# Two transposes two steps later, start-up tables in the mixing's memory, and a split last scatter in a two-layer encoder

## The chip, the cores and the metric

The kernel runs on one core of one Trainium2 chip. A core has TensorE (PE in the profile; PEld is its weight load), VectorE (DVE), ScalarE (ACT), GpSimd (POOL), SyncE (SP, which here only issues transfers) and 16 DMA engines. The metric is the device time of one execution in microseconds (us), from its start to its end, taken as the median of several runs.

## The reference

The reference is a streaming encoder of two layers (`DEPTH = 2`) over 256 tokens of width 1024, one sequence, all in float32. Each layer does this, cut to what matters:

```
mod = silu(c) @ w_ada[i] + b_ada[i]                 # 6 x 1024: sh1, sc1, g1, sh2, sc2, g2
h   = rmsnorm(x, norm1_g) * (1 + sc1) + sh1
q_a,k_a,v_a,u_s,q_r,k_r,v_r,g_r = split(h @ w_in)    # 1024 -> 2816 columns
y_a = chunk-banded attention, 8 heads, clipped relative bias
y_s = S5: complex diagonal recurrence over the tokens, discretised from
      a_re, a_im, exp(log_dt), then gelu and a GLU
y_r = 4-head retention with rotary angles, group norm, silu gate
x   = x + g1 * (concat(y_a, y_s, y_r) @ w_out)
h   = rmsnorm(x, norm2_g) * (1 + sc2) + sh2
x   = x + g2 * moe(h)      # 32 experts in 4 groups; best group, its best 2 experts
                           # expert: (silu(h @ gate) * (h @ up)) @ down, inner width 256
```

After the second layer a last RMSNorm gives the output. The S5 part needs, once per layer, the functions of its parameters: `exp(lam*dt)`, `(exp(lam*dt) - 1)/lam` and sines and cosines of the angle of each state at each token.

## The kernel before

**Tiling.** The 256 tokens are two blocks of 128 partitions, and `x` stays on the core as a 128x2x1024 tile. Large matrices come in pieces of 1 MB into a ring of slots (tiles named `w`, and `ring` in the mixture), issued in program order by SP: a load that must wait for its slot holds up every load behind it. The products of the mixing split both operands into a high and a low part (`wh`, twice per piece: line 767 on ScalarE makes the high part, line 768 on VectorE the low part) and add three matmuls.

**Start.** `x` and the constants are loaded, and eight 1 MB pieces of `w_ada` stream in. TensorE multiplies them as they land (line 231). Meanwhile `s5_prep` (lines 431 to 490) works out the S5 tables: some hundred VectorE instructions on 128x16 tiles (the range reduction of lines 369 and 370 and 411 to 414, the polynomial of 386 to 388), sines on ScalarE (418, 419), and two pairs of 128x256 tables named `fine` and `crs`. In its middle it calls `between()`, which gives ScalarE the four squared row sums of `x` (line 343). From these follow the mean square (347, 348), the inverse root (POOL at 335, VectorE at 337 to 339), the normed `x` in tiles named `early` (363 on VectorE, 364 on ScalarE), and its transposes on TensorE (855). The memory of `s5_prep` is a phase of its own, "prep", which ends before the phase "mix" begins.

**Mixing.** Five pieces of `w_in` products, the output product of attention and the rest run as steps g = 0, 1, 2, ...; `at(g, f)` hangs a further piece of work f on step g, and so the S5 recurrence, the retention, the attention and the next pieces of `w_ada` (line 231 whole, line 255 in halves) stand between the products of TensorE. That order is written out for TensorE and POOL; VectorE and ScalarE get theirs from a scheduler, which prefers what stands under `tc.high_priority`. When the `w_ada` half-row j = 11 is done, line 271 adds the bias to the row (128x256, VectorE), and `half_biased` (lines 282 to 287) transposes it by two matmuls (285) and copies columns of the result into `modT` (286), which is read by the norm ahead of the mixture. `at(g + 1, ...)` sets the step of `half_biased`.

**Mixture.** Each layer runs 16 rounds of two or four experts: gather of the tokens (1259), gate and up products (1297), Silu (1301), the product with the gate's weight (1303), transposes (1309), down products (1325) into two halves of 512 columns, the multiplication by `g2` (1338) and the scatter of the rows back to tokens (1356, 1358), added to `x` (1360). In the last round (`end`), `down` does all products of column half 0, then `outputs` and `scatter` of that half, two token blocks t = 0 and 1, then the same of half 1. Then comes the next layer, or `final` (1487 to 1504).

Of the kernel before, what the change touches and what calls it, by code (L numbers as in the profile page):

```python
# [15 lines left out]
AF = mybir.ActivationFunctionType  # L16
# [37 lines left out]
def body(tc, I, O):  # L54
# [3 lines left out]
    with tc.tile_pool(name="cp", bufs=1) as cp, tc.tile_pool(name="ring", bufs=NW) as ring, \  # L58
# [203 lines left out]
        def half_slot(l, i):  # L262
            h = i // 4
            if i % 4 == 0:
                ada_acc[l, 2] = ps("ac")
                bias_row[l, 2] = half_bias(l, h, sb([128, 512], "bad")[:, 0:256])
            acc = ada_acc[l, 2]
            half_mm(acc, i, load_half(l, i))
            if i == 3:
                row = ada_acc[l, 2] = y2([128, 512])[:, 0:256]  # L270
                V.tensor_tensor(row, acc[:, 0:256], bias_row.pop((l, 2)), op=ALU.add)
            if i == 7:
                half_gate(l, acc, bias_row.pop((l, 2)), y2([128, 512])[:, 0:256])
# [22 lines left out]
        def ada_gate(l, acc):  # L296

            row = y2([128, 512])
            V.tensor_tensor(row, acc, bias_row.pop((l, 1)), op=ALU.add)
            gr = gates[l, 1] = b4([128, 1024])  # L300
            for h in range(2):
                o = 32 * h
                A.dma_start(gr[:, h * 512:(h + 1) * 512], row[o:o + 32, :].unsqueeze(1).to_broadcast([32, 4, 512]))
            return row
# [69 lines left out]

        def expm1(src, w, tag):

            xx = sb([128, w], tag + "x")
            V.tensor_scalar(xx, src, -87.3, 88.0, op0=ALU.max, op1=ALU.min)
            n = sb([128, w], tag + "n")
            round_(n, xx, 1.4426950408889634)  # L380
            V.scalar_tensor_tensor(xx, n, -LN2H, xx, op0=ALU.mult, op1=ALU.add)
            V.scalar_tensor_tensor(xx, n, -LN2L, xx, op0=ALU.mult, op1=ALU.add)
            q = sb([128, w], tag + "q")
# [9 lines left out]
            em1 = sb([128, w], tag + "em1")  # L393
            V.tensor_tensor(em1, q, p2, op=ALU.mult)
            pm1 = sb([128, w], tag + "pm1")
            V.tensor_scalar(pm1, p2, -1.0, None, op0=ALU.add)
            V.tensor_tensor(em1, em1, pm1, op=ALU.add)
            ex = sb([128, w], tag + "ex")
# [32 lines left out]
        def s5_prep(between):  # L431
            ldt = C("ldt")
            _, dt = expm1(ldt, 16, "e1")
            live = sb([128, 16], "live")
            V.tensor_scalar(live, ldt, -87.3, None, op0=ALU.is_ge)
            V.tensor_tensor(dt, dt, live, op=ALU.mult)
            zr = sb([128, 16], "zr")
            V.tensor_tensor(zr, C("are"), dt, op=ALU.mult)
            phi = sb([128, 16], "phi")
            V.tensor_tensor(phi, C("aim"), dt, op=ALU.mult)  # L440
            n = sb([128, 16], "pn")
            ph = sb([128, 16], "ph")
# [3 lines left out]
            sn = sb([128, 16], "psn")  # L446
            cs = sb([128, 16], "pcs")
            hf = sb([128, 16], "phf")
            sincos(sn, cs, ph, hf)
            between()  # L450

            nr = sb([128, 16], "nr")
            ni = sb([128, 16], "nni")
# [4 lines left out]
            m2 = sb([128, 16], "m2")  # L458
            t = sb([128, 16], "m2t")
# [4 lines left out]
            t2 = sb([128, 16], "m2t2")  # L464
# [9 lines left out]
            ph16 = sb([128, 16], "ph16")  # L474
            V.tensor_scalar(phi, ph, 16.0, None, op0=ALU.mult)
            mod2pi(ph16, phi, n)
            t16 = sb([128, 16], "t16")
# [334 lines left out]
        def mixing(l, pre, xn, r4):  # L812
            todo = collections.defaultdict(list)

            def at(g, f, *args):
                todo[g].append((f, args))
# [12 lines left out]
            with tc.manual_schedule(engines={mybir.EngineType.PE}):  # L829
# [78 lines left out]
                for j in range(early_ada, n_ada):  # L908
                    g = 2 + int((j - early_ada) * 36 / (n_ada - early_ada))
                    at(g, ada_slot, l, j)  # L910
                    if j == 7:
                        at(g + 1, lambda: ada_biased(l, 1, ada_acc[l, 1]))
                    if j == 11:
                        at(g + 1, lambda: half_biased(l, ada_acc[l, 2]))
# [299 lines left out]
        def experts(posm, comb, xhi, xlo, a2, sh2, l, ahead=True, D0=None, between=None, order=None, more=True,  # L1214
# [72 lines left out]
            def gate_up(r, cw, mid=None):  # L1287
# [12 lines left out]
                si = b1_([128, 256])  # L1300
                A.activation(si, gu[:, 0:256], AF.Silu)  # L1301
                act = b1_([128, 256])
                V.scalar_tensor_tensor(act, gu[:, 256:512], cw, si, op0=ALU.mult, op1=ALU.mult)  # L1303
# [10 lines left out]
            def down(r, aT, end=False):  # L1314
                _, _, w, _, _, es = rounds[r]
                yp = [ps("sc") for _ in range(2)]
# [5 lines left out]
                for h, f, j in [(h, f, j) for h in range(2) for f in range(2) for j in range(len(es))] if ahead else \  # L1322
# [5 lines left out]
                    if end and (f, j) == (1, len(es) - 1):  # L1328

                        ys = outputs(yp, True, (h,))  # L1330
                        scatter(end, ys, h)
# [17 lines left out]
            def scatter(sT, ys, h0=0):  # L1349
                for h, (yh, yl) in enumerate(ys, h0):  # L1350
                    hs = slice(h * 512, (h + 1) * 512)
                    for t in range(2):
# [160 lines left out]
        with phase("prep"):  # L1513
            s5_prep(lambda: all_squares(ss0, ps("mm")))
        for l in range(L):
            more = l + 1 < L
            with phase("mix"):

                early()
# [124 lines left out]
```

## Time and profile before

| what | value |
|---|---|
| median of 3 runs | 843.98 us (843.56 to 847.43) |
| the profiled execution's own time | 842.86 us |
| its span, first to last instruction | 841.1 us (1.76 us lie outside) |
| TensorE busy | 716.7 us, 85% of the span |
| VectorE busy | 499.4 us, 59% |
| ScalarE busy | 252.0 us, 30% |
| GpSimd busy | 112.4 us, 13% |
| moved by DMA | 293.66 MB, mean 349 GB/s |
| mean granted TensorE clock | 0.951 of full speed |

A busy share is a mean over stages that have different limits: a wait counts only where the engine that waits is the one that the stage's end hangs on. An idle time in square brackets stands behind the first instruction after it, with the instruction that ended it.

### The profile page before, as it was taken

To read this page: it belongs to the slowest core of one execution; us is meant where nothing else is said; L and a number is where in the kernel's file an instruction comes from. 1 tells how busy PE (TensorE), PEld (TensorE's weight loads), DVE (VectorE), ACT (ScalarE), POOL (GpSimd) and SP (SyncE) were. 2 spreads that over 40 slices of the span, in tenths; PEclk is the share of its full clock that TensorE was granted. 3 is DMA by queue.
4 is the path that set the end of the run, shared out by engine and by line. 5 is a ranking of instruction groups with operands and counts; after the bars stand their busy time and mean duration, and the time that the engine had idled before them with its cause. 6 is when DMAs were issued, how large, how long until landed. Compare 5 with 4: busy or idle time off the path is not lost. (4 is left out here: it accounts for less than half of the span.)

```text
span 841.1 us, 12059 instructions
## 1 busy us (share of the span) xinstructions
PE 716.7 (85%) x4386; PEld 400.6 (48%) x4386; DVE 499.4 (59%) x1146; ACT 252.0 (30%) x541; POOL 112.4 (13%) x165
## 2 busy tenths in 40 slices
PE   3599979899999988598869799689989998869894
PEld 0265757675344443334227478467624344233431
DVE  4689997558555363425359989764865536252533
ACT  2343425934021121111135233394402112111112
POOL 0453160001000000000037215000000000000000
PEclk9599999999999999799999989899999999989998
DMA  9978779898999999999999754659869999989994
GB/s 372 421 269 315 272 284 340 287 376 345 417 420 415 418 416 371 389 409 419 404 413 420 280 168 141 228 216 382 324 216 420 417 415 420 414 334 414 418 411 155
DMA packets 57256, 293.66 MB, mean 349 GB/s; under 512 B 5088, under 2 KB 6880, under 8 KB 33888
## 3 DMA queue, kind: packets, MB, share of 16 engines
q1 hardware_dynamic: 54176, 288.23, 86.5%
q10 hardware_dynamic: 3008, 4.54, 1.6%
q8 instruction: 38, 0.62, 0.3%
q14 instruction: 34, 0.28, 0.1%
HBM read 289.60 MB, written 1.05 MB: 346 GB/s over the span
## 5 line engine op out<-in xcount | busy, mean ns | idle before, releaser
L1297 PE MATMUL mm<-ring,hg 128*32 128x512 f32 (+1 forms) x624 | 108.9, 595 | 0.9 <-DMA ring<-in_wgu_dram 0.9
L767 ACT ACTIVATE wh<-w 128x512 fp32r<-128x512 f32 x120 | 74.5, 630 | 98.8 <-PE mm L792 55.0
L768 DVE TENSOR_TENSOR wh<-w,wh 128x512 fp32r<-128x512 f32 x120 | 85.7, 736 | 28.3 <-ACT wh L767 27.9
L1303 DVE SCALAR_TENSOR_TENSOR b<-mm,cw,b 128x256 f32<-128x256 f32 x24 | 11.6, 483 | 141.2 <-ACT b L1301 141.2
L1297 PE MATMUL mm<-w,hg 128*64 128x512 f32 (+1 forms) x400 | 92.2, 612 | 0.0
L792 PE MATMUL mm<-wh,early 128*128 128x512 f32 x288 | 81.1, 426 | 3.7 <-DVE wh L768 3.6
L1325 PE MATMUL sc<-ring,b 128*64 128x512 f32 (+1 forms) x344 | 69.8, 597 | 1.2 <-ACT b L1311 1.1
L792 PEld LDWEIGHTS mm<-wh,early 128*128 128x128 f32 x288 | 54.7, 200 | 26.3 <-issue 6.6
L1301 ACT ACTIVATE b<-mm 128x256 f32<-128x256 f32 x24 | 9.2, 385 | 172.6 <-PE mm L1297 172.6
L1297 PEld LDWEIGHTS mm<-ring,hg 128*32 128x32 f32 (+1 forms) x624 | 30.9, 119 | 56.6 <-issue 53.3
L1343 ACT ACTIVATE y<-y 128x512 fp32r<-128x512 f32 x44 | 27.7, 629 | 92.4 <-DVE y L1338 92.4
L787 PE MATMUL mm<-early,wh 128*128 128x256 f32 x384 | 51.3, 287 | 2.5 <-DVE wh L768 2.5
L1338 DVE TENSOR_TENSOR y<-sc,gr 128x512 f32<-128x512 f32 x48 | 33.2, 692 | 32.8 <-PE sc L1325 27.0
L1275 POOL TENSOR_TENSOR b<-D,comd 128x128 f32<-128x128 f32 x32 | 12.5, 411 | 292.6 <-PE tr L1280 116.3
L1297 PEld LDWEIGHTS mm<-w,hg 128*64 128x64 f32 (+1 forms) x400 | 27.3, 134 | 50.6 <-issue 49.9
L787 PEld LDWEIGHTS mm<-early,wh 128*128 128x128 f32 x384 | 47.0, 189 | 6.4 <-DVE wh L768 3.0
L1259 PE MATMUL tr<-D,big 128*128 128x256 f32 x192 | 34.7, 323 | 16.8 <-DVE D L1210 15.4
L792 PE MATMUL mm<-wh,big 128*128 128x512 f32 x192 | 47.7, 399 | 1.4 <-DVE y L998 1.4
L231 PE MATMUL ac<-w,cc 128*32 128x512 f32 x192 | 29.1, 691 | 20.3 <-DVE cc L225 10.7
L1259 PEld LDWEIGHTS tr<-D,big 128*128 128x128 f32 x192 | 29.1, 217 | 25.6 <-issue 20.4
L1345 DVE TENSOR_TENSOR y<-y,y 128x512 fp32r<-128x512 f32 x44 | 30.3, 689 | 17.8 <-ACT y L1343 17.5
L792 PEld LDWEIGHTS mm<-wh,big 128*128 128x128 f32 x192 | 35.0, 188 | 9.3 <-DVE y L998 2.2
(367 smaller groups left out, 1161.6 us busy)
## 6 DMA issues: line engine op xcount, KB each, us to landing
ring<-in_wgu_dram SPq DMA_DIRECT2D x78, 1024.0 KB, 16.5
w<-in_wgu_dram SPq DMA_DIRECT2D x50, 1024.0 KB, 14.5
w<-in_w_ada_dram SPq DMA_DIRECT2D x36, 1024.0 KB, 9.1
ring<-in_moe_w_down_dram SPq DMA_DIRECT2D x36, 1024.0 KB, 19.9
w<-in_win_dram SPq DMA_DIRECT2D x22, 1024.0 KB, 7.7
w<-in_moe_w_down_dram SPq DMA_DIRECT2D x20, 1024.0 KB, 17.4
ring<-in_w_ada_dram SPq DMA_DIRECT2D x12, 1024.0 KB, 7.9
w<-in_w_out_dram SPq DMA_DIRECT2D x8, 1024.0 KB, 7.2
```

The lines of the kernel that those rows point to most:

```text
L231: PE.matmul(acc[32 * t:32 * t + 32, :], c1[:, k:k + 1].to_broadcast([128, 32]), w[:, t * 512:(t + 1) * 512], start=(k == 0), stop=(k == 7) ...
L767: A.activation(wh[:, 0], w, AF.Copy)
L768: lo_eng[par_[0] % len(lo_eng)].tensor_tensor(wh[:, 1], w, wh[:, 0].bitcast(F32), op=ALU.subtract)
L787: PE.matmul(pt[t][:, f * 256:(f + 1) * 256], whs[i][:, w_, fs], a[x_][:, k], start=first and f + m == 0, stop=end and m == 2, skip_group_c ...
L792: PE.matmul(pt[t], a[x_][:, k, ts_], whs[i][:, w_], start=first and m == 0, stop=end and m == 2)
L1259: PE.matmul(pc[c], (xlo if i else xhi)[:, t, cs], Dm[blk][:, t, ss], start=(i + t == 0), stop=(i + t == 3))
L1275: G.tensor_tensor(Dc[:, t].rearrange("p (e s) -> p e s", s=w), Dm[blk][:, t, po:po + 128].bitcast(F32).rearrange("p (e s) -> p e s", s=w), ...
L1297: PE.matmul(gu[o:o + w, :], hg[blk, k][:, po + o:po + o + w], ws[k // 4][j][:, k % 4] if ahead else part_gu(l, es[j], k), start=(k == 0), ...
L1325: PE.matmul(yp[h][o:o + w, :], aT[:, f * 128 + o:f * 128 + o + w], wd[h][f][j] if ahead else part_wd(l, es[j], f, h), start=(f == 0), stop ...
L1338: V.tensor_tensor(y, yp[h], gates[l, 2][:, h * 512:(h + 1) * 512], op=ALU.mult)
L1343: A.activation(yh, y, AF.Copy)
L1345: V.tensor_tensor(yl, y, yh.bitcast(F32), op=ALU.subtract)
```

## The change

Four things change. (1) `half_biased` is hung two steps later, and the two row additions that feed it and its sister (`half_slot`, `ada_gate`) get high priority. (2) The small tiles of `s5_prep` are cut from one 128x512 tile (`s16`), `s5_prep` runs inside the phase "mix" of layer 0, the unused first `early()` tile of each layer goes, and the squares are tied by a small copy to the cosine `cs`, so that they come after it. (3) Silu and the product behind it get high priority. (4) In the last round of a layer the scatter of half 0 is split: its block t = 0 stands between the products f = 0 and f = 1 of half 1, its block t = 1 after both.

The diff, with the many lines left out in which `sb([128, w], ...)` or `sb([128, 16], ...)` becomes `s16()`:

```
@@ half_slot / ada_gate
-                V.tensor_tensor(row, acc[:, 0:256], bias_row.pop((l, 2)), op=ALU.add)
+                with tc.high_priority(offset=PRIO):
+                    V.tensor_tensor(row, acc[:, 0:256], bias_row.pop((l, 2)), op=ALU.add)
...
-            V.tensor_tensor(row, acc, bias_row.pop((l, 1)), op=ALU.add)
+            with tc.high_priority(offset=PRIO):
+                V.tensor_tensor(row, acc, bias_row.pop((l, 1)), op=ALU.add)
@@ s5_prep
+        small = []
+        def s16():
+            if not small:
+                t = y2([128, 512])
+                small.extend(t[:, i * 16:(i + 1) * 16] for i in range(32))
+            return small.pop(0)
...
             sincos(sn, cs, ph, hf)
-            between()
+            between(cs)
@@ mixing
-                        at(g + 1, lambda: half_biased(l, ada_acc[l, 2]))
+                        at(g + 3, lambda: half_biased(l, ada_acc[l, 2]))
@@ gate_up
-                si = b1_([128, 256])
-                A.activation(si, gu[:, 0:256], AF.Silu)
-                act = b1_([128, 256])
-                V.scalar_tensor_tensor(act, gu[:, 256:512], cw, si, op0=ALU.mult, op1=ALU.mult)
+                si, act = b1_([128, 256]), b1_([128, 256])
+                with tc.high_priority(offset=PRIO):
+                    A.activation(si, gu[:, 0:256], AF.Silu)
+                    V.scalar_tensor_tensor(act, gu[:, 256:512], cw, si, op0=ALU.mult, op1=ALU.mult)
@@ down
-                    if end and (f, j) == (1, len(es) - 1):
-                        ys = outputs(yp, True, (h,))
-                        scatter(end, ys, h)
+                    if end and j == len(es) - 1:
+                        if f == 1:
+                            ye[h] = outputs(yp, True, (h,))
+                        if h == 1:
+                            scatter(end, ye[0], 0, (f,))
+                            if f == 1:
+                                scatter(end, ye[1], 1)
@@ scatter(sT, ys, h0=0, ts=(0, 1))
-                    for t in range(2):
+                    for t in ts:
@@ main
-        with phase("prep"):
-            s5_prep(lambda: all_squares(ss0, ps("mm")))
+        def first_squares(cs):
+            scr = ps("mm")
+            V.tensor_copy(scr[:, 0:1], cs[:, 0:1])
+            all_squares(ss0, scr)
         for l in range(L):
             with phase("mix"):
-                early()
+                if l == 0:
+                    s5_prep(first_squares)
```

**ScalarE at the start.** These are its instructions from the second transfer on; `mm` is the squares' scratch tile, `ss` their sums, `ph` the S5 angle, `early` the normed `x`. Before:

```order
L222 ACT_TABLE_LOAD
L222 ACTIVATE cth<-cst 128x8 [waits DMAHW0_49]
L343 ACTIVATE mm_200,ss_104<-x 128x512 [waits DMAHW2_49]
L343 ACTIVATE mm_200,ss_104<-x 128x512 [waits Activation_49] x3
L418 ACT_TABLE_LOAD
L418 ACTIVATE psn_193<-ph_152 128x16 [waits DVE_49]
L419 ACTIVATE phf_195<-ph_152 128x16
L418 ACTIVATE fine_s<-b_42_236 128x256 [waits DVE_49]
L419 ACTIVATE b_43_237<-b_42_236 128x256
L418 ACTIVATE crs_s<-b_45_250 128x256 [waits DVE_49]
L419 ACTIVATE b_46_251<-b_45_250 128x256
L364 ACTIVATE early_272<-x,rry_280 128x512 [waits DVE_49,Activation_49]
```

and with the change:

```order
L222 ACT_TABLE_LOAD
L222 ACTIVATE cth<-cst 128x8 [waits DMAHW0_49]
L429 ACT_TABLE_LOAD
L429 ACTIVATE y_11_111<-y_11_111 128x16 [waits DVE_49]
L430 ACTIVATE y_11_111<-y_11_111 128x16
L345 ACTIVATE mm_181,ss_104<-x 128x512 [waits DMAHW2_49,DVE_49]
L345 ACTIVATE mm_181,ss_104<-x 128x512 [waits Activation_49] x3
L429 ACTIVATE fine_s<-b_16_211 128x256 [waits DVE_49]
L430 ACTIVATE b_17_212<-b_16_211 128x256
L366 ACTIVATE early_238<-x,rry_246 128x512 [waits DVE_49]
L366 ACTIVATE early_238<-x,rry_246 128x512
L429 ACTIVATE crs_s<-b_19_225 128x256 [waits DVE_49]
```

The table load and the two small sines stand ahead of the squares now, and the normed `x` ahead of the `crs` tables; on VectorE its half of `early` moves in the same way, from behind the last `crs` instruction to a place ahead of both tables' cosines.

**TensorE in layer 1's mixing.** `tr` takes the transposes of the half row `y`, `mm` a product of a `w_in` piece's part `wh`. Before, the end of one part, the transposes, and the next part:

```order
L792 MATMUL mm_7207<-wh_7231,early_6278 128x512 x2
L792 MATMUL mm_7207<-wh_7231,early_6279 128x512
L285 MATMUL tr_7240<-cst,y_1942_7229 128x128 [waits DVE_49]
L285 MATMUL tr_7240<-cst,y_1942_7229 128x128
L792 MATMUL mm_7206<-wh_7244,early_6278 128x512 x2
```

and with the change, where the transposes stand now:

```order
L589 MATMUL ac_6929<-b_1857_6819,par_6190 32x256
L589 MATMUL ac_6929<-b_1890_7040,par_6190 32x256
L589 MATMUL ac_6929<-b_1893_7051,par_6190 32x256
L286 MATMUL tr_7265<-cst,y_1912_7194 128x128 x2
L803 MATMUL mm_7171<-wh_7271,early_6243 128x512 [waits Activation_49]
```

The two transposes moved behind two further parts' products, the scores of one attention step and the S5 output matmuls (line 578 of before); on VectorE the row addition moved two instructions up. In layer 0 they moved behind one further part, two other transposes (748) and half of the next part.

**TensorE in the last round of layer 1.** `sc` takes the down products of half 1, `ac` the scatter of half 0, `tr` that of half 1. Before:

```order
L1356 MATMUL ac_11994<-y_3403_11992,sT_11864 128x512 [waits DVE_49]
L1356 MATMUL ac_11997<-y_3403_11992,sT_11864 128x512
L1325 MATMUL sc_11967<-ring_3401_11970,b_3396_11964 32x512 [waits DMAHW2_49,PE_49]
L1325 MATMUL sc_11967<-ring_3401_11970,b_3396_11964 32x512 [waits DMAHW3_49]
L1325 MATMUL sc_11967<-ring_3401_11970,b_3396_11964 32x512 [waits DMAHW4_49]
L1325 MATMUL sc_11967<-ring_3401_11970,b_3396_11964 32x512 [waits DMAHW5_49]
L1325 MATMUL sc_11967<-ring_3402_11971,b_3396_11964 32x512 [waits DMAHW6_49]
L1325 MATMUL sc_11967<-ring_3402_11971,b_3396_11964 32x512 [waits DMAHW7_49]
L1325 MATMUL sc_11967<-ring_3402_11971,b_3396_11964 32x512 [waits DMAHW0_49]
L1325 MATMUL sc_11967<-ring_3402_11971,b_3396_11964 32x512 [waits DMAHW1_49]
L1356 MATMUL tr_12010<-y_3406_12008,sT_11864 128x512 [waits DVE_49]
L1356 MATMUL tr_12013<-y_3406_12008,sT_11864 128x512
```

and with the change:

```order
L1336 MATMUL sc_11932<-ring_3371_11935,b_3366_11929 32x512 [waits DMAHW2_49,PE_49]
L1336 MATMUL sc_11932<-ring_3371_11935,b_3366_11929 32x512 [waits DMAHW3_49]
L1336 MATMUL sc_11932<-ring_3371_11935,b_3366_11929 32x512 [waits DMAHW4_49]
L1336 MATMUL sc_11932<-ring_3371_11935,b_3366_11929 32x512 [waits DMAHW5_49]
L1371 MATMUL ac_11963<-y_3373_11957,sT_11829 128x512 [waits DVE_49]
L1336 MATMUL sc_11932<-ring_3372_11936,b_3366_11929 32x512 [waits DMAHW6_49]
L1336 MATMUL sc_11932<-ring_3372_11936,b_3366_11929 32x512 [waits DMAHW7_49]
L1336 MATMUL sc_11932<-ring_3372_11936,b_3366_11929 32x512 [waits DMAHW0_49]
L1336 MATMUL sc_11932<-ring_3372_11936,b_3366_11929 32x512 [waits DMAHW1_49]
L1371 MATMUL ac_11972<-y_3373_11957,sT_11829 128x512
L1371 MATMUL tr_11975<-y_3375_11970,sT_11829 128x512 [waits DVE_49]
L1371 MATMUL tr_11978<-y_3375_11970,sT_11829 128x512
```

Four of the eight products moved ahead of the scatter's first block and four between its two blocks; layer 0 has the same. In the mixture's other rounds, Silu and its product stand where they stood.

## Rows read from the trace of the kernel before

**Rows 1.** The page: busy us, share of the span, instructions of each engine.
```profile
PE 716.7 (85%) x4386; PEld 400.6 (48%) x4386; DVE 499.4 (59%) x1146; ACT 252.0 (30%) x541; POOL 112.4 (13%) x165
```

**Rows 2.** Cores: span, mean granted TensorE clock.
```profile
core 0: 841.1 us, clock 0.951
```

**Rows 3.** Windows: us, busy of PE, PEld, DVE, ACT, POOL; PEclk, DMA share, GB/s.
```profile
205.00:460.00 255.00, 221.03 (x1253) 102.02 (x1252) 127.72 (x246) 55.88 (x109) 31.65 (x49) 0.96 1.01 410
...
625.00:825.00 200.00, 175.99 (x1006) 77.94 (x1002) 83.57 (x152) 34.46 (x66) 7.75 (x20) 0.97 1.00 407
```

**Rows 4.** Waits, whole span: engine, line, waited for; us in total, times, longest.
```profile
PE tr L285 <- DVE y L271: 8.5, 2, 5.5
```

**Rows 5.** Timeline of the start: start us, us, instruction, [idle before <-releaser].
```profile
17.18 1.28 ACT L418 ACT_TABLE_LOAD   x1
17.19 0.16 DVE L347 TENSOR_TENSOR ssv<-ss 128x2 f32<-128x2 f32 x1 [3.03 <-ACT mm L343]
...
18.82 0.17 DVE L420 TENSOR_TENSOR phf<-phf 128x16 f32<-128x16 f32 x1 [1.39 <-ACT phf L419]
...
24.88 1.93 PE L231 MATMUL ac<-w,cc 128*32 128x512 f32 x8 [0.55 <-DMA w<-in_w_ada_dram]
...
28.69 1.71 DVE L363 TENSOR_SCALAR early<-x,rry 128x512 f32<-128x512 f32 x2
...
29.68 1.97 PE L855 MATMUL sc<-cst,early 128*128 128x128 f32 x8 [2.87 <-DVE early L363]
...
33.29 1.62 PE L231 MATMUL ac<-w,cc 128*32 128x512 f32 x8
```

**Rows 6.** Timeline of layer 0's mixing, from the half row's addition.
```profile
124.57 0.42 DVE L271 TENSOR_TENSOR y<-ac,bad 128x256 f32<-128x256 f32 x1
...
125.05 0.44 PE L285 MATMUL tr<-cst,y 128*128 128x128 f32 x2 [2.98 <-DVE y L271]
...
140.08 0.69 DVE L768 TENSOR_TENSOR wh<-w,wh 128x512 fp32r<-128x512 f32 x1 [1.91 <-ACT wh L767]
```

**Rows 7.** Timeline of layer 1's mixing, the same place and what follows.
```profile
539.02 0.69 PE L285 MATMUL tr<-cst,y 128*128 128x128 f32 x2 [5.48 <-DVE y L271]
...
539.36 2.91 PE L792 MATMUL mm<-wh,early 128*128 128x512 f32 x6
...
542.97 0.69 DVE L768 TENSOR_TENSOR wh<-w,wh 128x512 fp32r<-128x512 f32 x1 [2.85 <-ACT wh L767]
...
543.45 1.66 PE L792 MATMUL mm<-wh,early 128*128 128x512 f32 x6
543.66 0.42 DVE L633 CUSTOM_DVE_ANT_0 y<-sc,r 128x256 f32<-128x256 f32 x1
```

**Rows 8.** Windows of the same place (columns as in rows 3).
```profile
533.60:539.00 5.40, 0.00 (x0) 0.00 (x0) 5.40 (x11) 0.63 (x1) 0.00 (x0) 0.74 0.54 184
539.00:545.00 6.00, 5.98 (x22) 4.20 (x22) 2.79 (x12) 2.52 (x4) 0.00 (x0) 0.66 0.61 209
```

**Rows 9.** Timeline of layer 0's end.
```profile
429.17 0.69 DVE L1360 TENSOR_TENSOR x<-x,tr 128x512 f32<-128x512 f32 x1 [0.17 <-PE tr L1356]
...
430.39 1.06 PE L231 MATMUL ac<-w,cc 128*32 128x512 f32 x8 [1.26 <-DMA w<-in_w_ada_dram]
```

**Rows 10.** Timeline of the last round of layer 1.
```profile
822.44 1.92 PE L1325 MATMUL sc<-ring,b 128*32 128x512 f32 x16 [0.53 <-ACT b L1311]
...
825.18 1.98 PE L1356 MATMUL ac<-y,sT 128*128 128x512 f32 x4 [0.81 <-DVE y L1338]
...
827.09 1.92 PE L1325 MATMUL sc<-ring,b 128*32 128x512 f32 x16
...
829.16 0.69 DVE L1338 TENSOR_TENSOR y<-sc,gr 128x512 f32<-128x512 f32 x1
...
831.93 0.69 DVE L1360 TENSOR_TENSOR x<-x,tr 128x512 f32<-128x512 f32 x1 [0.17 <-PE tr L1356]
```

**Rows 11.** Window in that round (columns as in rows 3).
```profile
826.00:827.00 1.00, 1.00 (x3) 0.19 (x1) 0.66 (x1) 0.00 (x0) 0.00 (x0) 1.00 0.29 111
```

More of the change, by code (lines that the diff above doesn't have):

```diff
@@ L373, in body @@
         COEF = [1.0 / 5040, 1.0 / 720, 1.0 / 120, 1.0 / 24, 1.0 / 6, 0.5, 1.0]
+        small = []
[4 more added lines that the diff above has]
+            return small.pop(0)
         def expm1(src, w, tag):
-            xx = sb([128, w], tag + "x")
+            xx = s16()
             V.tensor_scalar(xx, src, -87.3, 88.0, op0=ALU.max, op1=ALU.min)
-            n = sb([128, w], tag + "n")
+            n = s16()
             round_(n, xx, 1.4426950408889634)
@@ L382, in expm1 @@
             V.scalar_tensor_tensor(xx, n, -LN2L, xx, op0=ALU.mult, op1=ALU.add)
-            q = sb([128, w], tag + "q")
+            q = s16()
             V.tensor_scalar(q, xx, 1.0 / 40320, COEF[0], op0=ALU.mult, op1=ALU.add)
@@ L392, in expm1 @@
             p2 = ni.bitcast(F32)
-            em1 = sb([128, w], tag + "em1")
+            em1 = s16()
             V.tensor_tensor(em1, q, p2, op=ALU.mult)
-            pm1 = sb([128, w], tag + "pm1")
+            pm1 = s16()
             V.tensor_scalar(pm1, p2, -1.0, None, op0=ALU.add)
             V.tensor_tensor(em1, em1, pm1, op=ALU.add)
-            ex = sb([128, w], tag + "ex")
+            ex = s16()
             V.tensor_scalar(ex, q, 1.0, None, op0=ALU.add)
@@ L433, in s5_prep @@
             _, dt = expm1(ldt, 16, "e1")
-            live = sb([128, 16], "live")
+            live = s16()
             V.tensor_scalar(live, ldt, -87.3, None, op0=ALU.is_ge)
             V.tensor_tensor(dt, dt, live, op=ALU.mult)
-            zr = sb([128, 16], "zr")
+            zr = s16()
             V.tensor_tensor(zr, C("are"), dt, op=ALU.mult)
-            phi = sb([128, 16], "phi")
+            phi = s16()
             V.tensor_tensor(phi, C("aim"), dt, op=ALU.mult)
-            n = sb([128, 16], "pn")
-            ph = sb([128, 16], "ph")
+            n = s16()
+            ph = s16()
             mod2pi(ph, phi, n)
@@ L445, in s5_prep @@
             V.tensor_copy(radius, ex)
-            sn = sb([128, 16], "psn")
-            cs = sb([128, 16], "pcs")
-            hf = sb([128, 16], "phf")
+            sn = s16()
+            cs = s16()
+            hf = s16()
             sincos(sn, cs, ph, hf)
-            between()
-            nr = sb([128, 16], "nr")
-            ni = sb([128, 16], "nni")
+            between(cs)
+            nr = s16()
+            ni = s16()
             V.tensor_tensor(nr, em1, cs, op=ALU.mult)
@@ L456, in s5_prep @@
             V.tensor_tensor(ni, ex, sn, op=ALU.mult)
-            m2 = sb([128, 16], "m2")
-            t = sb([128, 16], "m2t")
+            m2 = s16()
+            t = s16()
             V.tensor_tensor(m2, C("are"), C("are"), op=ALU.mult)
@@ L463, in s5_prep @@
             V.reciprocal(m2, m2)
-            t2 = sb([128, 16], "m2t2")
+            t2 = s16()
             V.tensor_tensor(t, nr, C("are"), op=ALU.mult)
@@ L472, in s5_prep @@
             V.tensor_tensor(co_im, t, m2, op=ALU.mult)
-            ph16 = sb([128, 16], "ph16")
+            ph16 = s16()
             V.tensor_scalar(phi, ph, 16.0, None, op0=ALU.mult)
             mod2pi(ph16, phi, n)
-            t16 = sb([128, 16], "t16")
+            t16 = s16()
             V.tensor_scalar(t16, C("iota")[:, 0:16], -1.0, None, op0=ALU.add)
@@ L1315, in down @@
                 _, _, w, _, _, es = rounds[r]
-                yp = [ps("sc") for _ in range(2)]
+                yp, ye = [ps("sc") for _ in range(2)], {}
                 if ahead and end:
@@ L1347, in outputs, with scatter @@
                 return out
-            def scatter(sT, ys, h0=0):
+            def scatter(sT, ys, h0=0, ts=(0, 1)):
                 for h, (yh, yl) in enumerate(ys, h0):
                     hs = slice(h * 512, (h + 1) * 512)
-                    for t in range(2):
+                    for t in ts:
                         p = ps(("ac", "tr")[h])
```

## Prediction

> **What bounds the kernel now.** I read the page first, then windows by stage, then the waits, then the timeline around each edited place. The page shows TensorE busy in 85% of the span and VectorE in 59% [rows 1], but no one engine bounds the whole. In the two mixtures the windows show the DMA engines at a share of 1.01 and 1.00, 410 and 407 GB/s, with TensorE busy in 221.03 of 255 us and in 175.99 of 200 [rows 3]: there the transfer of weights and TensorE run side by side, each near its limit. In the mixings no engine is full all the time; their length is a chain that goes from TensorE to VectorE and ScalarE and back, and what can be gained there are waits of TensorE on that chain. The waits name one that belongs to an edited line: TensorE's transposes of line 285 wait 8.5 us for the row addition of line 271, twice [rows 4]. Ahead of layer 0 TensorE waits 2.87 us for the normed `x` [rows 5], and the last round of a layer runs its two halves one after the other [rows 10]. So the change works at five places, and the sum goes place by place.
>
> **The start.** ScalarE squares `x` before it loads the Sin table, and VectorE stands still twice for it: 3.03 us until the squares end and 1.39 us until the small sines do [rows 5]. Then it works through the tables without a gap worth much until 28.69, when it norms `x`; TensorE takes that up at 29.68, 2.87 us after the seventh piece of `w_ada` was done (24.88 + 1.93 = 26.81) [rows 5]. With the change the Sin load (1.28) and the sines need only the angle; the squares follow; the two stalls shrink, and the norm no longer stands behind the cosines. Taking 3 to 4 us of stall and about 3 us of table work out of its way puts `early` near 22, some 5 us before TensorE can use it. TensorE is then held by the seventh piece alone, which comes from memory at its own rate, so the gain is the whole wait and no more: -2.8 us, for everything behind (the eighth piece, 33.29 [rows 5], and the modulation). The table work put off hides beside the transposes, in which VectorE has nothing to norm. From both sides: no better than -2.9, and if the postponed tables hold up the modulation, half: -1.4. The small tiles in one memory add no instruction; the copy to the scratch tile is one of 128x1, at most the 0.17 of the small VectorE instructions [rows 5], ahead of squares that have 5 us to spare. It costs nothing, or 0.2 if that cover is gone.
>
> **Layer 0's mixing.** The transposes wait 2.98 us [rows 6]. Two steps later the part of `w_in` that followed, two transposes and half a part come first; what they read was made earlier, and they fill the time until the addition has ended (124.57 + 0.42). What is late next is VectorE, which was full during the wait; behind it it has 1.91 us free in one gap at 140.08 [rows 6] and smaller ones, so TensorE's lead is kept, less a little: -2.6. Bounds: -1.0, if VectorE can give only half of its gap, and -3.0.
>
> **Layer 1's mixing.** The same wait lasts 5.48 us; VectorE is busy 5.40 of the 5.40 us in it, TensorE 0.00, and the granted clock is 0.74 in it and 0.66 in the six us behind [rows 7, 8]. There the six matmuls of one part take 2.91 us, the next six of the same form 1.66 [rows 7]. With the transposes behind two parts, a score step and the S5 matmuls, TensorE runs these during the wait. VectorE's own work does not shrink, and that sets the gain: it is free at 542.97 - 2.85 = 540.12, and then waited for ScalarE, which waited for TensorE's products; the softmax of the step comes at 543.66 [rows 7]. With the products done in time it can begin at about 540.1. The gain is 543.66 - 540.1 = 3.5 us. Upper end: wait, slow matmuls and nothing in return, 5.48 + (2.91 - 1.66) + 0.4 for the slower scores, estimated from the same clock, = 7.1. Lower end: the wait comes back on VectorE and only the slow part's 1.2 is won. I take -3.5, since VectorE's row decides it. The row addition moves up by two instructions and delays these by its 0.41; that is inside this value.
>
> **Ends of the layers.** Half 0's scatter is four matmul entries in 1.98 us, 0.99 per token block, and each half's products take 1.92, 0.96 per f [rows 10]. Now half 1's f = 0 starts when half 0's products end (822.44 + 1.92 = 824.36) and fills the time in which VectorE multiplies; block 0 goes at 825.3, f = 1 at 826.3, ready at 827.3 where it was 827.09 + 1.92 = 829.01. VectorE has an addition and, in layer 1, one product of the final norm (0.69 each, as its other 128x512 instructions [rows 10]) ahead of the multiplication, which then starts near 827.9 in place of 829.16 [rows 10]: -1.3. But the last weights are still landing: the DMA share is 0.29 between 826 and 827 [rows 11], so the last products of f = 1 may wait up to half a us: -0.8. Bounds -1.3 and, if the stream is 2 us later against TensorE than now, +1.0 (TensorE, in order, then holds block 1 too). In layer 0 the same shape, but what follows is another piece of `w_ada` that TensorE awaits from memory until 430.39, 1.2 us after the last addition began [rows 9]: about half gets through, -0.7, between 0 and -1.3.
>
> **Silu and its product** stand where they stood in every round: 0.
>
> **Sum.** 2.8 + 2.6 + 0.7 + 3.5 + 0.8 = 10.4 us off the profiled execution's 842.86: 832.5. The median of the runs is 1.1 above that execution, so 833.6 on its basis. All lower ends together give 843.98 - 2.6 = 841.4, all upper ends 843.98 - 15.6 = 828.4.
>
> **Rivals.**
> *B, swallowed by the stream.* The DMA share of 1.00 in both mixtures [rows 3] can mean that a mixture ends when its bytes have come. What TensorE wins in front of it would then turn into waits for weights, and only what lies behind the last weights counts: -0.7 and -0.8, thus 842.5. Against it: the stream is released by TensorE and VectorE finishing the mixing, since weights take the slots that these free, so it starts earlier when they do.
> The Trainium skill, "Perfetto Trace Analysis", section Roofline, puts the practical ceiling of one core's transfers at about 435 GB/s, some 120% of its 358 GB/s share, and calls a kernel latency-bound only where both matmul and memory use are low. The 410 GB/s of the row agrees with the ceiling; by the page's rule the mixtures are bound by transfers and the mixings, with gaps in both, by latency, and the time would be B's or my forecast according to whether the stream's start moves.
>
> *C, VectorE takes over.* In the waits VectorE was full [rows 8]; if its work follows on everywhere, the two mixings and the start give half: (2.8 + 2.6 + 3.5) / 2 + 1.5 = 6.0, 838.0. For it: 5.40 of 5.40. Against it: the gaps of 2.85 and 1.91 right behind [rows 6, 7].
>
> *D, slower: the granted clock.* The mean is 0.951 [rows 2], and 0.66 where matmuls follow the wait [rows 8]. Should the denser order bring lower grants over the mixtures, 716.7 us of matmuls [rows 1] cost 716.7 x 0.951 / 0.93 - 716.7 = 16 us at a mean of 0.93: 849. It decides from a mean of about 0.937, where it eats the 10.4. Against it: the lower grants shown stand behind a stretch in which TensorE did nothing, and the change removes such stretches.
>
> *E, the moves don't help:* the transposes wait again at their new place, or the norm comes no earlier. The order speaks against it for the first (the addition now stands ahead of what the S5 matmuls wait for); price 842.5 with the ends alone, and it shares B's time.
>
> **How the numbers follow.** Forecast 0.68, C 0.14, B and E together 0.13, D 0.05. About 0.5% (4.2 us) is what a measurement of this kernel can tell from no change, so faster means below 839.8 and slower above 848.2. The forecast and C are faster (0.82), B and E within (0.13), D slower (0.05). The forecast's own range is 828 to 838; to leave out no more than two in ten it reaches toward B: 827.5 to 841.
>
> **What would show it.** Right: the line-285 transposes gone from the waits; the first transposes of `early` at about 26.9, released by the seventh piece; the softmax of layer 1 some 3.5 us earlier against its neighbours and no clock of 0.66 behind it; the mixtures of the same length as now, begun earlier; the last addition 0.8 us closer to the last gate product. Wrong: a mixture longer by what its mixing lost (B), a VectorE wait of the old size under another name (C), or a lower mean clock at the same instructions (D).

## The result, and the profile after

The changed kernel takes 830.53 us (median of 4 runs, 829.75 to 831.48) where the kernel before, beside it, takes 843.81: a ratio of 0.9846, 95% interval 0.9824 to 0.9867, 13.3 us less. Two further sets of five runs beside the kernel before gave 0.9838 (0.9810 to 0.9865) and 0.9837 (0.9808 to 0.9866). The profiled execution took 831.48 us, the longest of its four, so the two traces have 842.86 - 831.48 = 11.4 us between them.

The page and the cores after (against [rows 1, 2]):

```profile
PE 714.2 (86%) x4386; PEld 402.4 (49%) x4386; DVE 498.2 (60%) x1147; ACT 252.1 (30%) x541; POOL 112.1 (14%) x165
```
```profile
core 0: 829.7 us, clock 0.955
```

The work is the same but for one small VectorE copy; what differs are the waits and the granted clock (a row's 1.00 is the upper of its two levels, 0.50 the lower; a value between them is a mean of both). The two mixtures, in windows of the same length as in [rows 3]:

```profile
202.00:457.00 255.00, 223.13 (x1263) 104.83 (x1263) 130.33 (x250) 56.40 (x109) 31.63 (x49) 0.96 1.01 409
614.00:814.00 200.00, 176.03 (x1013) 78.80 (x1010) 83.54 (x152) 34.48 (x66) 7.75 (x20) 0.97 1.00 407
```

They run at the rate of before. To see where the time went I set the same matmul's start in both traces side by side; the difference is how far the changed kernel is ahead:

| place (line before) | before, us | after, us | difference |
|---|---|---|---|
| first transposes of `early` (855) | 29.68 | 26.69 | -2.99 |
| transposes for the modulation (316) | 35.64 | 30.94 | -4.70 |
| layer 0, ahead of the wait (255) | 112.02 | 108.03 | -3.99 |
| layer 0, part behind the wait (787) | 125.24 | 117.60 | -7.64 |
| layer 0, retention's second pair (748) | 128.78 | 124.49 | -4.29 |
| layer 0, a few parts on (787) | 132.05 | 130.31 | -1.74 |
| layer 0's mixture, first gathers (1259) | 206.49 | 204.62 | -1.87 |
| layer 0's mixture, second gate product (1297) | 220.96 | 218.01 | -2.95 |
| layer 0's mixture, late (1297) | 417.06 | 413.93 | -3.14 |
| layer 1's mixing, behind the first steps (792) | 457.19 | 453.09 | -4.10 |
| layer 1, part ahead of the wait (792) | 532.12 | 525.63 | -6.49 |
| layer 1, first turned softmax (646) | 550.87 | 538.07 | -12.80 |
| layer 1's mixture (1259) | 604.26 | 593.78 | -10.48 |
| the same, late (1259) | 755.38 | 744.67 | -10.70 |
| end of the span | 841.1 | 829.7 | -11.4 |

Two of the steps in this table lie where nothing was edited. At the start of layer 0's mixture the lead goes from 1.87 to 3.57 us, and early in layer 1's mixing from 4.10 to 6.49. Each pair of windows, first of before, then of after, holds the same matmuls; the granted clock (third number from the end) was lower in the trace of before:

```profile
206.49:228.00 21.51, 19.48 (x89) 7.54 (x90) 14.60 (x45) 3.94 (x7) 1.20 (x2) 0.92 1.01 419
457.19:497.76 40.57, 34.54 (x173) 24.17 (x172) 37.28 (x68) 14.13 (x27) 10.59 (x13) 0.87 0.66 243
```
```profile
204.62:224.43 19.81, 17.78 (x89) 7.13 (x90) 14.59 (x45) 3.94 (x7) 1.20 (x2) 1.00 1.01 419
453.09:491.27 38.18, 31.59 (x173) 22.23 (x172) 37.03 (x68) 14.03 (x27) 10.54 (x13) 0.96 0.73 269
```

So 1.7 and 2.4 us of the lead are TensorE running the same products at a higher grant. Part of the first goes again later: the lead is 3.08 us at the last Silu of that mixture (417.75 against 414.67).

**The start**, timeline (against [rows 5]):

```profile
19.72 0.88 DVE L365 TENSOR_SCALAR early<-x,rry 128x512 f32<-128x512 f32 x2
...
24.82 1.94 PE L231 MATMUL ac<-w,cc 128*32 128x512 f32 x8 [0.55 <-DMA w<-in_w_ada_dram]
...
26.69 1.67 PE L866 MATMUL sc<-cst,early 128*128 128x128 f32 x8
...
29.16 1.06 PE L231 MATMUL ac<-w,cc 128*32 128x512 f32 x8
```

The norm comes 9 us earlier, and the transposes follow the seventh piece at once. The eighth piece takes 1.06 us where it took 1.62 [rows 5]. The windows from the first transposes to those for the modulation, first of before, then of after, show why: TensorE is busy 5.23 us at a granted clock of 0.60, and 3.53 us at 0.86.

```profile
29.68:35.64 5.96, 5.23 (x24) 3.49 (x25) 0.71 (x1) 1.00 (x2) 5.57 (x9) 0.60 1.02 418
```
```profile
26.69:30.94 4.25, 3.53 (x28) 2.46 (x24) 0.00 (x0) 0.60 (x1) 4.01 (x7) 0.86 1.02 425
```

**Layer 0's mixing** (against [rows 6]), timeline and window:

```profile
120.41 0.44 PE L286 MATMUL tr<-cst,y 128*128 128x128 f32 x2 [0.28 <-DVE y L272]
...
123.83 0.60 DVE L765 SCALAR_TENSOR_TENSOR big<-tr,hgn,big 128x128 fp32r<-128x128 f32 x2
...
124.49 0.69 PE L759 MATMUL tr<-cst,b 128*128 128x128 f32 x2 [2.64 <-DVE big L765]
```
```profile
113.00:129.00 16.00, 13.08 (x105) 10.95 (x104) 15.55 (x30) 3.52 (x8) 1.56 (x3) 0.83 0.88 321
```

The old wait of 2.98 is 0.28; a new one of 2.64 stands four us later. The tag `tr` has two banks: the retention's first pair of transposes holds one until line 765 has emptied it, the half row now takes the other, and the second pair finds none. That is read from the order and the wait; l0_later5 below tests it. From the matmul at 112.02 before to that at 132.74 (line 255 both times) TensorE has the same work in both kernels, and the stretch got longer:

```profile
112.02:132.74 20.72, 15.76 (x148) 12.81 (x147) 20.62 (x38) 5.96 (x12) 6.26 (x9) 1.00 0.76 287
```
```profile
108.03:130.99 22.96, 18.38 (x147) 15.34 (x146) 21.18 (x37) 6.01 (x12) 6.04 (x8) 0.85 0.70 257
```

**Layer 1's mixing** (against [rows 7, 8]), timeline and windows:

```profile
531.84 1.09 PE L589 MATMUL ac<-b,par 128*32 128x256 f32 x15
...
533.60 0.42 DVE L644 CUSTOM_DVE_ANT_0 y<-sc,r 128x256 f32<-128x256 f32 x1
...
533.95 0.44 PE L286 MATMUL tr<-cst,y 128*128 128x128 f32 x2
```
```profile
527.00:533.60 6.60, 5.87 (x52) 3.71 (x51) 6.60 (x14) 2.55 (x3) 0.00 (x0) 1.00 0.60 211
533.60:539.00 5.40, 5.40 (x33) 3.94 (x29) 4.97 (x20) 4.41 (x14) 0.00 (x0) 1.00 0.99 390
```

VectorE is full in the first window as it was in the wait, TensorE now works beside it, and the clock is 1.00 in both windows, where it was 0.74 and 0.66 [rows 8]. Further on a part goes again: at a later softmax that TensorE turns it waits 1.40 us for ScalarE, first after, then the same transpose before, for which the trace lists no wait:

```profile
546.35 0.33 PE L657 MATMUL tr<-cst,y 128*128 128x128 f32 x1 [1.40 <-ACT y L652]
```
```profile
557.70 0.33 PE L646 MATMUL tr<-cst,y 128*128 128x128 f32 x1
```

**The last round** (against [rows 10]), timeline:

```profile
811.29 3.53 PE L1336 MATMUL sc<-ring,b 128*32 128x512 f32 x24 [0.53 <-ACT b L1322]
...
813.78 0.14 PEld L1336 LDWEIGHTS sc<-ring,b 128*32 128x32 f32 x2 [0.54 <-DMA ring<-in_moe_w_down_dram]
...
814.75 1.13 PE L1371 MATMUL ac<-y,sT 128*128 128x512 f32 x2
...
815.81 1.57 PE L1336 MATMUL sc<-ring,b 128*32 128x512 f32 x8
...
816.33 0.14 PEld L1336 LDWEIGHTS sc<-ring,b 128*32 128x32 f32 x2 [0.37 <-DMA ring<-in_moe_w_down_dram]
...
819.80 1.28 DVE L1375 TENSOR_TENSOR x<-x,tr 128x512 f32<-128x512 f32 x2
```

From the first down product to the end of the last addition it takes 9.8 us (811.29 to 819.80 + 1.28); before 10.2 (822.44 to 831.93 + 0.69 [rows 10]). TensorE waits for weights twice, 0.54 and 0.37 us, in the two groups of half 1's products.

### The profile page after: what moved, and what is told of

The parts are those of the page before. It is cut to its first block, busy times and chain, and to the rows that moved or that the text cites. A ratio compares the mean times of both kernels' runs of the same rounds, so it can differ in the third digit from the quotient of the medians.

```text
span 829.7 us, 12062 instructions
## 1 busy us (share of the span) xinstructions
PE 714.2 (86%) x4386; PEld 402.4 (49%) x4386; DVE 498.2 (60%) x1147; ACT 252.1 (30%) x541; POOL 112.1 (14%) x165
## 5 line engine op out<-in xcount | busy, mean ns | idle before, releaser
L803 PE MATMUL mm<-wh,early 128*128 128x512 f32 x288 | 77.9, 413 | 4.3 <-DVE wh L779 4.1
L803 PEld LDWEIGHTS mm<-wh,early 128*128 128x128 f32 x288 | 52.6, 192 | 25.9 <-DVE wh L779 6.5
L798 PE MATMUL mm<-early,wh 128*128 128x256 f32 x384 | 53.5, 296 | 2.1 <-DVE wh L779 2.1
L798 PEld LDWEIGHTS mm<-early,wh 128*128 128x128 f32 x384 | 49.4, 199 | 6.1 <-DVE wh L779 2.7
L1336 PEld LDWEIGHTS sc<-ring,b 128*64 128x64 f32 (+1 forms) x344 | 19.9, 122 | 40.6 <-issue 33.8
```

The source lines that it names most:

```text
L798: PE.matmul(pt[t][:, f * 256:(f + 1) * 256], whs[i][:, w_, fs], a[x_][:, k], start=first and f + m == 0, stop=end and m == 2, skip_group_c ...
L803: PE.matmul(pt[t], a[x_][:, k, ts_], whs[i][:, w_], start=first and m == 0, stop=end and m == 2)
L1336: PE.matmul(yp[h][o:o + w, :], aT[:, f * 128 + o:f * 128 + o + w], wd[h][f][j] if ahead else part_wd(l, es[j], f, h), start=(f == 0), stop ...
```

## The experiments

Each kernel ran beside the kernel before; a ratio below 1 is faster. The third column is the median over a kernel's runs of the mean granted clock; the kernel before has 0.949 in 59 runs, the changed kernel 0.957 in 14.

| kernel | ratio to before (95%) | clock | median, before, difference (us) |
|---|---|---|---|
| start_only | 0.9932 (0.9907 to 0.9956) | 0.953 | 838.25, 843.58, -5.3 |
| turn_only | 0.9955 (0.9935 to 0.9974) | 0.951 | 838.80, 843.58, -4.8 |
| scatter_only | 0.9980 (0.9964 to 0.9995) | 0.950 | 842.19, 843.58, -1.4 |
| turn_bank | 0.9870 (0.9845 to 0.9894) | 0.959 | 832.98, 843.58, -10.6 |
| after_again | 0.9838 (0.9810 to 0.9865) | 0.957 | 830.38, 844.39, -14.0 |
| layer1_turn | 0.9853 (0.9828 to 0.9879) | 0.954 | 832.00, 844.39, -12.4 |
| l0_later5 | 0.9812 (0.9784 to 0.9841) | 0.954 | 828.46, 844.39, -15.9 |
| squares_late | 0.9952 (0.9930 to 0.9973) | 0.948 | 840.90, 844.39, -3.5 |
| after_third | 0.9837 (0.9808 to 0.9866) | 0.959 | 830.87, 844.14, -13.3 |
| l0_again | 0.9804 (0.9776 to 0.9832) | 0.955 | 828.96, 844.14, -15.2 |
| mem_only | 0.9928 (0.9902 to 0.9953) | 0.953 | 837.65, 844.14, -6.5 |
| prio_only | 0.9979 (0.9963 to 0.9995) | 0.950 | 842.74, 844.14, -1.4 |

**start_only**: part (2) of the diff alone on the kernel before, its core:

```
-        with phase("prep"):
-            s5_prep(lambda: all_squares(ss0, ps("mm")))
+                if l == 0:
+                    s5_prep(first_squares)    # in phase "mix", small tiles from s16()
```

> The kernel before with the start part alone (tables' small tiles in the mixing's memory, no dummy tile, squares behind the cosine). Theory: the first product of the mixing comes 4.8 us earlier, as in the changed kernel's trace, and layer 0's mixing passes that on: 4 to 5 us less than before, about 839.3. Rival (VectorE bounds layer 0's mixing, so an earlier start is given back there): in the changed kernel only 1.7 of 4.7 us were left at the middle of that mixing, so 1 to 2 us less, about 842.3.

5.3 us less, so by time the rival is out. In the trace the lead is about 3.8 us from 48 to 109 us and 4.1 at 125; it falls to 2.7 at 131 and to 1.1 at 168, and in both places this trace's clock is lower than before's (0.91 against 1.00 from 112 to 132 us, 0.62 against 0.81 from 154 to 163). It is 2.4 at layer 0's end and 5.3 to 6.7 in layer 1's mixture, after 2.4 us won where the trace of before has the clock of 0.87 shown above. So behind the start the lead comes and goes with the granted clock; no row shows VectorE taking it back.

**mem_only** and **squares_late** split that part. mem_only is start_only without one line:

```
-            V.tensor_copy(scr[:, 0:1], cs[:, 0:1])
```

> The kernel before with the tables' small tiles in the mixing's memory and the dummy tile gone, but the squares ahead of the sines as before (no copy). Theory (either half of the start's edit is enough): the two VectorE stalls of 3.03 and 1.39 us stay, but the normed x no longer waits for the last table and is ready near 21, so the first transposes start at 26.7, released by the seventh piece: 4 to 5.5 us less than before. Rival (the stalls are what counts): the transposes stay behind 28, under 1 us less.

6.5 us less. Its timeline keeps the stalls, and the norm stands ahead of the tables:

```profile
17.26 0.16 DVE L347 TENSOR_TENSOR ssv<-ss 128x2 f32<-128x2 f32 x1 [3.01 <-ACT mm L343]
...
18.89 0.18 DVE L429 TENSOR_TENSOR y<-y 128x16 f32<-128x16 f32 x1 [1.39 <-ACT y L428]
...
20.75 0.88 DVE L363 TENSOR_SCALAR early<-x,rry 128x512 f32<-128x512 f32 x2
...
24.63 1.93 PE L231 MATMUL ac<-w,cc 128*32 128x512 f32 x8 [0.55 <-DMA w<-in_w_ada_dram]
...
26.50 1.85 PE L864 MATMUL sc<-cst,early 128*128 128x128 f32 x8
```

squares_late adds that copy to the kernel before and moves no memory:

```
-            s5_prep(lambda: all_squares(ss0, ps("mm")))
+            s5_prep(first_squares)
```

> The kernel before with the squares tied behind the cosine by the small copy, nothing else: the tables keep their own memory and the normed x stays behind the last table. Theory (either half of the start's edit is enough, since TensorE is held by the seventh piece until 26.7): the two VectorE stalls go, the norm comes about 4 us earlier, near 25, and the first transposes start at 26.7 as with the whole start part: 4 to 5.5 us less than before. Rival (the memory is what counts): the norm stays near 28, under 1 us less.

3.5 us less. Here the stalls are gone, and the norm stays behind the last table:

```profile
13.88 0.17 DVE L420 TENSOR_TENSOR phf<-phf 128x16 f32<-128x16 f32 x1
...
17.65 0.15 DVE L347 TENSOR_TENSOR ssv<-ss 128x2 f32<-128x2 f32 x1
...
24.05 1.71 DVE L363 TENSOR_SCALAR early<-x,rry 128x512 f32<-128x512 f32 x2
...
24.83 1.90 PE L231 MATMUL ac<-w,cc 128*32 128x512 f32 x8 [0.55 <-DMA w<-in_w_ada_dram]
...
26.66 1.09 PE L858 MATMUL sc<-cst,early 128*128 128x128 f32 x8
```

Each half alone brings the transposes to 26.5 to 26.7, where the seventh piece ends. Nothing was left there for the other half: either edit would have done. The times agree with that as far as they can: 6.5, 3.5 and 5.3 for both together have intervals of about 2 us each. (3.5 is a little under what was expected; most runs of this kernel had a mean clock of 0.945 to 0.950.)

**turn_only** and **prio_only**: part (1) alone, and its two `high_priority` lines without the step:

```
-                        at(g + 1, lambda: half_biased(l, ada_acc[l, 2]))    # turn_only alone
+                        at(g + 3, lambda: half_biased(l, ada_acc[l, 2]))
+                with tc.high_priority(offset=PRIO):    # both kernels, at two row additions
```

> The kernel before with the half row's transposes two steps later and the row additions prioritised, nothing else. Theory: only layer 1's wait is won (5.5 us and its slow matmuls, together 6 to 6.5), layer 0's 3 us come back as a wait for one of the two transpose banks: 6 to 7 us less, about 837.3, with a TensorE wait of 2 to 3 us ahead of the retention's second pair of transposes in layer 0. Rival (as predicted blind): both waits are won in part, 2.6 and 3.5 us: 6.1 less, 837.7, without that new wait; the wait tells them apart, not the time. Rival 2 (the weights' stream swallows what is won): under 1.5 us less, 842.5.

4.8 us less, somewhat under 6 to 7. In the trace TensorE is 1.4 us ahead in front of layer 1's wait (532.12 against 530.74), 7.7 behind it and mostly 6.1 to 7.1 in the mixture: 6.3 won at the wait, 4.7 to 5.7 of it kept. In layer 0 the bank's wait was only 0.55 us in this trace (of a weight load), not 2 to 3, because TensorE came late: its matmuls ran at half the clock from 118 to 125 us (the S5 products of eight matmuls took 2.08 us, against 1.13 in the changed kernel's trace), and so gained nothing either.

> The kernel before with the two row additions at high priority, the transposes at their old step. Theory (the step is what counts, VectorE being full in layer 1's wait): the addition moves up by two instructions of 0.68 us in layer 1 and by one of 0.42 or so in layer 0, so the transposes wait that much less: 1 to 2 us less than before. Rival (the priority alone does it): 4 us less or more.

1.4 us less. The transposes still wait, 4.28 us in layer 1 (5.48 before [rows 7]) and 2.66 in layer 0 (2.98 [rows 6]): the step is what counts.

```profile
124.55 0.44 PE L286 MATMUL tr<-cst,y 128*128 128x128 f32 x2 [2.66 <-DVE y L272]
...
538.39 0.69 PE L286 MATMUL tr<-cst,y 128*128 128x128 f32 x2 [4.28 <-DVE y L272]
```

**scatter_only**: part (4) alone, in `down`:

```
-                        ys = outputs(yp, True, (h,))
-                        scatter(end, ys, h)
+                            scatter(end, ye[0], 0, (f,))
+                            if f == 1:
+                                scatter(end, ye[1], 1)
```

> The kernel before with the split scatter of the last round alone. Theory: 0.9 us at the kernel's end and 0.5 to 1.2 at layer 0's end: 1.4 to 2.1 us less, about 842.1. Rival (last weights land too late for the moved products): under 0.5 us less, or more than before by up to 1.

1.4 us less; the theory holds at its lower end, though the interval, 0.4 to 3.0 us, hardly excludes the rival. The trace bears the theory out: against before it wins about 0.55 us at layer 0's end (from 1.20 behind to 0.65) and 0.4 in the last round.

**turn_bank**: the changed kernel with another bank for the half row.

```
         def half_biased(l, row):
-            tp = ps("tr")
+            tp = ps("ac")
```

> The changed kernel with the half row's transposes in an accumulator bank of the tag ac in place of tr; nothing else. Theory: the retention's second pair of transposes no longer waits for the bank that the first pair's evacuation (line 765) frees late, so layer 0's mixing loses its 2.6 us wait: 2 to 2.6 us less than the changed kernel, about 828.3. Rival (VectorE, full in that stretch, sets the pace): the wait moves to the next weight part's low half, less than 0.8 us off, about 830.

Neither: 10.6 us less than before, no better than the changed kernel. The wait moved and grew. The next half row's accumulator wants a bank of `ac`, and VectorE copies the half row out late:

```profile
120.75 0.44 PE L286 MATMUL ac<-cst,y 128*128 128x128 f32 x2 [0.28 <-DVE y L272]
126.17 1.93 PE L255 MATMUL ac<-w,cc 128*32 128x256 f32 x16 [4.99 <-DVE modT L287]
128.04 0.69 PE L759 MATMUL tr<-cst,b 128*128 128x128 f32 x2
```

The second pair indeed no longer waits, but as a test of what sets the pace this decides nothing. **l0_later5** was made for that, with the changed kernel (**after_again**) and **layer1_turn** beside it, and run a second time as **l0_again** beside **after_third**.

```
                         at(g + 3, lambda: half_biased(l, ada_acc[l, 2]))    # changed kernel
                         at(g + (3 if l else 1), lambda: half_biased(l, ada_acc[l, 2]))    # layer1_turn
                         at(g + (3 if l else 5), lambda: half_biased(l, half_row[l]))    # l0_later5
```

> The changed kernel itself, so that the next two can be compared with it on one chip. The same as before: about 830.5, 13 us less than before.

> The changed kernel with layer 0's transposes two steps later still, behind the retention's second pair of transposes and two further parts, from a row kept by name; layer 1 as changed. The two banks then serve the retention's pairs alone. Theory (the bank sets layer 0's pace): the wait of 2.64 us ahead of the second pair goes and nothing takes its place: 2 to 2.6 us less than the changed kernel. Rival (VectorE, which is full from 113 to 129 us, sets it): TensorE waits as long for the low half of the next weight part; within 0.8 us of the changed kernel.

> The changed kernel once more, as the neighbour of the next run on one chip: about 830.5.

> The changed kernel with layer 0's transposes behind the retention's second pair, once more, since its 1.9 us against the changed kernel lay inside both intervals. Theory (the bank's wait was on the path): 2 to 2.6 us less than the changed kernel beside it, about 828.2. Rival (the 1.9 us were scatter of the granted clock): within 0.8 us of it.

1.92 and 1.91 us less than the changed kernel beside it. The trace of l0_again has neither wait:

```profile
121.11 1.07 PE L255 MATMUL ac<-w,cc 128*32 128x256 f32 x16 [0.27 <-DVE y L274]
122.11 0.44 PE L761 MATMUL tr<-cst,b 128*128 128x128 f32 x2
122.31 3.83 PE L800 MATMUL mm<-early,wh 128*128 128x256 f32 x30
```

The two intervals overlap those of the changed kernel in each set. The means of the runs differ by 1.6 and 2.6 us, together 2.1 with a 95% interval of about 1.5, worked out from the scatter of the 12 and 10 runs. The traces say it more clearly. This is the stretch of equal work from above, in the traces of before, of the changed kernel, and of the kernels that differ from it in layer 0's transposes alone:

| where the transposes stand | trace: length of the stretch, us (granted clock) |
|---|---|
| old step | before 20.72 (1.00), layer1_turn 20.04 (1.00) |
| two steps later | after 22.96 (0.85), after_again 21.63 (0.92), after_third 21.92 (0.92) |
| behind the second pair | l0_later5 17.54 (1.00), l0_again 17.55 (1.00) |

```profile
108.74:126.29 17.55, 15.63 (x147) 12.79 (x147) 17.38 (x29) 6.05 (x13) 6.03 (x8) 1.00 0.71 259
```

VectorE is busy 17.38 of the 17.55 us, as full as before, and does the rest later (29 instructions here, 38 before); TensorE waits for it 1.65 and 0.27 us in this stretch, as in the changed kernel, and no more. The lead won is still there at 141 us. So the bank was what held TensorE, not VectorE's load. At 828.5 and 829.0 us this version beats both kernels.

> The changed kernel with layer 0's transposes back at their old step; layer 1's stay two steps later. Theory: in layer 0 the change turned the wait for the row addition into one for a transpose bank, so taking it back costs nothing: within 1 us of the changed kernel, with the transposes again waiting 2 to 3 us in layer 0 and the bank's wait gone. Rival (layer 0's shift is worth its 2.6 us): 2 to 3 us more than the changed kernel.

1.6 us more than the changed kernel, between theory and rival, with intervals that overlap: not settled by time. Its trace has the wait for the row back (2.63 us) and the bank's gone, and needs 20.04 us for the stretch in the table, less than the changed kernel in any of its three; so in the traces layer 0's shift costs rather than gains. Behind it the clocks differ: this trace loses 1.7 us early in layer 1's mixing, where after_again wins 2.4.

## Why the prediction was right, and where it was not

The forecast was 10.4 us off; 13.3 to 14.0 came. The direction was right, and the start and the two layer ends went for the reason given. That the sum came so near is partly luck: one term of 2.6 was lost, the start and layer 1 gave more than their terms, and some 3.6 us of the trace's 11.4 (1.87 to 3.08 and 4.10 to 6.49) came in stretches that no term covers, where the trace of before had the lower clock.

- **Start, -2.8: right mechanism, size too small.** The first transposes came at 26.69, released by the seventh piece, 2.99 us earlier against 2.8 forecast. What the sum missed is the granted clock: 0.60 in the stretch behind the transposes before, 0.86 after, so the transposes and the eighth piece took 1.7 us less as well. Together 4.7, of which 4.0 are left in front of layer 0's wait; start_only 5.3.
- **Layer 0's mixing, -2.6: the step that failed.** "What they read was made earlier" holds, but the step asked only for what the moved instructions read, not for what they write into. The wait of 2.98 us came back as one of 2.64 at the second pair, for a bank, and in all three traces of the changed kernel the clock fell to its lower level in that wait or behind it. The stretch got 0.9 to 2.2 us longer instead of 2.6 shorter, and the lead of 4.0 was 1.87 where the mixture began. VectorE's gap, on which I let the gain hang, was not the limit: with the transposes behind the second pair the same stretch is 3.2 us shorter than before. By time alone the term isn't settled (layer1_turn, 1.6 us).
- **Layer 0's end, -0.7:** the trace's lead grew from 3.1 to 3.5 at the next awaited piece and to 3.8 behind the transposes and the modulation's last piece (442.95 before, 439.14 after). Right.
- **Layer 1's mixing, -3.5: mis-sized.** The softmax gained 543.66 - 533.60 - 6.49 = 3.57 us, as forecast from VectorE's row. But TensorE's own queue gained 6.3 (12.80 - 6.49), since the parts that stood behind the wait at a clock of 0.66 were done. The new wait of 1.40 us for ScalarE took 1.25 of it (the lead falls from 12.59 to 11.34 there), and 4.0 to 4.4 arrived in the mixture, 4.7 to 5.7 in turn_only. So VectorE's row did not decide it alone; the term lies between 3.5 and TensorE's 6.3.
- **Last round, -0.8:** 0.4 in the trace. The weights' late landing, given as the reason for cutting 1.3 to 0.8, cost more: 0.54 and 0.37 us before two weight loads. scatter_only, both layers' ends together, 1.4, against 1.5 forecast.
- **Silu, 0:** ScalarE's and VectorE's instructions in layer 0's mixture have the same order in both traces, as forecast.
- **Rivals.** B fell: the lead does not shrink over a mixture, from -1.87 to -3.08 in layer 0's and from -10.48 to -10.70 in layer 1's, so these streams at a DMA share of 1.00 swallowed nothing; their start moved with TensorE. C fell in layer 1. In layer 0 its sign did come, a wait of the old size released by VectorE (line 765); but l0_later5 and l0_again, with VectorE as full and no such wait, show that the bank made it. D fell, the other way round: the clock rose. E: the transposes themselves wait 0.28 us at their new place, but in layer 0 later ones wait in their stead, so there its first half came true in substance; its price, the ends alone, did not.

The three parts alone (the fourth, Silu, moved nothing) give 5.3 + 4.8 + 1.4 = 11.5 us, the whole 13.3 to 14.0. The 1.8 to 2.5 us between them are not clear of noise: the intervals are about 2.1, 1.6 and 1.3 us for the parts and 1.8 to 2.5 for the whole. Nor does the mean clock explain them, since the parts' medians rise by 0.004, 0.002 and 0.001 over before, together nearly the whole's 0.008. What the clock itself is worth can only be estimated. The kernel before takes 844.8 us in its 24 runs at 0.947 or lower and 843.1 in 13 at 0.953 or higher; squares_late has a median of 842.9 in three runs at 0.945 and 837.0 in three at 0.958. By these two, the 0.008 between before and after go with some 1.5 to 3.6 us. That is worked out from the scatter of runs, not tested, and it doesn't say which is cause and which effect.

## What to carry to other kernels

When an instruction is moved to another place in an order, ask for three things: when what it reads is ready, what waits for its result, and whose buffer it takes; here, in a pool of two banks, a saved wait of 2.98 us came back as one of 2.64 a few instructions on. A gain in front of a stage that is full of transfers need not be lost in it; here it arrived behind both mixtures, whose transfers began earlier with the work in front of them. Where two edits free the same wait, try each alone: here either of them brought TensorE to the same start. And when two single traces are compared, look at the stretches that no edit touches as well: here they held some 3.6 us of the 11.4.

## What the runs showed of the hardware that was not expected

The mean granted clock differs from run to run of one kernel, 0.943 to 0.961 over 59 runs of the kernel before, with times from 840.4 to 848.7 us; differences of 2 us between two kernels need many runs, and a single trace shows its own clock. Removing waits of TensorE went with a higher mean, 0.949 to 0.957, rather than a lower one. But not every wait brings a lower grant: the stretch around the wait of 2.98 us in layer 0 ran at 1.00 before, the one around the bank's wait of 2.64 at 0.85 to 0.92.
